# Attention kernel, 1 core: issuing the query loads and the output projection's transfers from ScalarE's instruction stream and not from SyncE's

## The chip, the cores and the metric

The kernel runs on one core of one Trainium2 chip. The metric is the device time of one execution in microseconds (us). Before the change three runs gave a median of 1577.47 us (1572.33 to 1581.16).

Five engines work beside each other, each through its own list of instructions, strictly in the order of that list: PE (TensorE, the matmuls), DVE (VectorE), ACT (ScalarE), POOL (GpSimd) and SP (SyncE, which here only starts transfers). An instruction waits for the semaphores of what it depends on, and everything behind it on its engine waits with it. A transfer (DMA) is started by an instruction of one of these lists and then moves by itself on 16 DMA engines.

## The reference

One layer: RMSNorm and one input projection, whose columns go to four mixers of width 256, then an output projection and the residual. The sequences are 2048 and 512 tokens long; the model width is 1024.

```python
def _layer(x, cos, sin, norm_w, w_in, ..., w_out):
    proj = _rms_norm(x, norm_w) @ w_in
    (a_u, a_v, a_z, b_q, ..., c_q, c_k, c_v, c_z, d_x, d_z) = _split_cols(proj)
    y_a = _sgu_mixer(a_u, a_v, sgu_w, sgu_b) * jax.nn.silu(a_z)
    y_b = _deltanet_mixer(b_q, b_k, b_v, ...) * jax.nn.silu(b_z)
    y_c = _attention_mixer(c_q, c_k, c_v, ...) * jax.nn.silu(c_z)
    y_d = _pool_mixer(d_x, pool_w, pool_scale) * jax.nn.silu(d_z)
    mix = jnp.concatenate([y_a, y_b, y_c, y_d], axis=-1)
    return x + mix @ w_out
```

The attention is softmax(q k^T / 8) v over the whole sequence, with 4 query heads on 2 key heads of width 64.

## The kernel before

Tokens are cut into five blocks of 512 (b = 0 to 3 the long sequence, b = 4 the short one). Values are carried as pairs of float16, a high part and the rest, so that one product takes three matmuls. The program has three phases that overlap. Phase 1 projects and convolves, phase 2 computes the gates and the DeltaNet recurrence, and phase 3 (line 849 on) does attention and the output projection. What a later phase needs goes through DRAM: the queries as QS, the keys as KS, the mixer outputs as MIX (eight tiles for each block).

**Attention.** Work runs over (block, head). For one head, `load_q` (L867) loads the tiles qa and qb with three transfers. `row_max` (L874) computes the row maxima: matmuls mp (L884), DVE maxima (L886), a transposing matmul mr (L892), and an ACT copy into the last row of qb (L894). `attn` (L899) then runs over the key tiles, 16 for a long block and 4 for the short one. Each key tile is one score: two matmuls into a bank sp (L909, L910), the exponential e on ACT (L912), its float16 copy p on ACT (L915), the rest of p on DVE or, for one score in four, on POOL (L916), and twelve short matmuls O (L921). While head h is in `attn`, the maxima of head h+1 are woven in, one step for each score. The tiles qa and qb have two buffers each, so the load for head h+1 has to wait until the scores of head h-1 are done. Banks of sp: three.

**Output projection.** When all four heads of a block are through, `post` finishes the DeltaNet part, and `store_mix` (L1391) writes MIX tiles: an ACT copy (L1398), a DVE rest (L1399), a store (L1400). `outproj` (L940) then issues eight loads mx of the MIX tiles (L946). Its work is queued in units: after each score `pump` takes one unit, which is three matmuls op (L958), so op fills PE between scores. For each 128 tokens there are a load of the residual xr (L952), two DVE results y (L962) and a store of y (L967).

**Order.** The order on each engine is not written by hand. A scheduler simulates the program with its own model of time and puts each instruction into its engine's list at the moment when the model has it ready, by priority: attention high, output projection low. So moving a transfer to another engine can move any instruction after it. Transfers take turns on eight completion semaphores, whichever engine starts them, and each waits for the transfer that had its semaphore before.

Of the kernel before, what the change touches and what calls it, by code (L numbers as in the profile page):

```python
# [44 lines left out]
class Trunk:  # L45
# [802 lines left out]
    def phase3(self, kp, ap, wp, ep, e5, rest, post):  # L848


        tc, nc, I = self.tc, self.nc, self.I
        V, A, G, PE, NB = nc.vector, nc.scalar, nc.gpsimd, nc.tensor, self.NB
        if True:
# [12 lines left out]
            def load_q(b, h):  # L866
                qa = ap.tile([128, 512], F16, tag="qa", name="qa")  # L867
                qb = ap.tile([65, 512], F16, tag="qb", name="qb")
                for i in range(2):
                    nc.sync.dma_start(qa[i * 64:i * 64 + 64, :], self.QS[b][0, h])  # L870
                nc.sync.dma_start(qb[0:64, :], self.QS[b][1, h])
                return qa, qb

            def row_max(seq, b, h):  # L874

                s0, n, KA, KB, vt = seq
                q = qs[b, h] = load_q(b, h)
                qa, qb = q
                nsc = n // 512
                mm = ap.tile([128, 4, nsc], F32, tag="mm", name="mm")  # L880
                for qt in range(4):
                    for sc in range(nsc):
                        mp = self.bank("M" + w0(b), [128, 512], "mp")
                        PE.matmul(mp, qa[:, qt * 128:qt * 128 + 128], KA[h // 2][:, sc * 512:sc * 512 + 512],  # L884
                                  start=True, stop=True)
                        V.tensor_reduce(mm[:, qt, sc:sc + 1], mp, axis=AX.X, op=ALU.max)  # L886
                        yield
                m16 = ap.tile([128, 4], F16, tag="m16", name="m16")
                V.tensor_reduce(m16, mm, axis=AX.X, op=ALU.max, negate=True)
                mr = self.bank("M" + w0(b), [128, 512], "mr")  # L890
                for qt in range(4):
                    PE.matmul(mr[64:65, qt * 128:qt * 128 + 128], m16[:, qt:qt + 1], self.id16,  # L892
                              start=True, stop=True, tile_position=(0, 64))
                A.activation(qb[64:65, :], mr[64:65, :], AF.Copy)  # L894
# [46 lines left out]
            def outproj(b):  # L941
                mix = []
                for f in range(8):
                    p, tag, n = (pool5(), "mx5", 7) if b % 2 and f < 7 else (ep, "mx4", 1) if b % 2 else (ep, "mx3", 8)
                    m = p.tile([128, 2, 512], F16, tag=tag, name="mx3", bufs=n)
                    nc.sync.dma_start(m, self.MIX[b][f])  # L946
                    mix.append(m)
                def units():
                    for tt in range(4):
                        t0 = b * 512 + tt * 128  # L950
                        xr = ep.tile([128, 1024], F32, tag="xr", name="xr")
                        nc.sync.dma_start(xr, I["x"][t0:t0 + 128, :])  # L952
                        y = ep.tile([128, 1024], F32, tag="y", name="y")
                        for n in range(2):
                            op = self.bank("X" + str(max(0, b - NB + 3)), [128, 512], "op")
                            for i, k in enumerate((0, 1, 6, 7, 2, 3, 4, 5)):
                                for j, (a, c) in enumerate(((0, 0), (0, 1), (1, 0))):
                                    PE.matmul(op, mix[k][:, a, tt * 128:tt * 128 + 128], wo[k][:, c, n * 512:n * 512 + 512],  # L958
                                              start=i + j == 0, stop=i == 7 and j == 2)
                                if i < 7:  # L960
                                    yield
                            V.scalar_tensor_tensor(y[:, n * 512:n * 512 + 512], op, IWS / MS, xr[:, n * 512:n * 512 + 512],  # L962
                                                   op0=ALU.mult, op1=ALU.add)
                            if n == 0:
                                yield
                        dst = self.O[0][t0:t0 + 128, :] if t0 < self.NP else self.O[1][t0 - self.NP:t0 - self.NP + 128, :]
                        nc.sync.dma_start(dst, y)  # L967
                        yield

                queue.append((clock[0] + LAG, units()))  # L970
# [3 lines left out]
            def pool5():  # L974
                if not p5:
                    p5.append(e5())
                return p5[0]
# [39 lines left out]
            for i, w in enumerate(work):  # L1017
                with tc.high_priority(offset=2000000):
                    attn(*w, row_max(*work[i + 1]) if i + 1 < len(work) else iter(()))
                if w[2] == 3:  # L1020
                    with tc.high_priority(offset=3000000):
                        post(w[1])
                    outproj(w[1])
# [462 lines left out]
```

## Time and profile before

| | |
|---|---|
| median of three runs | 1577.47 us (1572.33 to 1581.16) |
| the profiled execution | 1574.01 us |
| its span, first to last instruction | 1572.2 us |
| PE busy over the span | 1425.8 us (91%) |
| DVE | 1173.3 us (75%) |
| ACT | 797.0 us (51%) |
| POOL | 546.7 us (35%) |
| hardware DMA queue | 267.36 MB |

The busy shares are averages over phases that have different limits. Starting a transfer isn't counted as busy, so the work that the change moves is in none of these rows. In the trace, SPq stands for SP's list and PEld for the loads of weights, which overlap with PE. What stands behind "idle before" or "waited for" is the engine or transfer whose semaphore came last.

### The profile page before, as it was taken

Reading aid. Unit: us, or ns where it says so; the run is one execution under the profiler, and the core shown is the slowest. Engines: PE = TensorE matmul, PEld = TensorE weight load, DVE = VectorE, ACT = ScalarE, POOL = GpSimd, SP = SyncE. Lnnn points to the kernel's source line nnn. Section 1 sums busy time; section 2 is a strip of 40 time slices with the busy share of each in tenths; the row PEclk is TensorE's granted clock in tenths of the full one; section 3 lists DMA queues with packets and bytes.
Section 4 is the critical chain, followed back from the end, with each engine's and each line's share of the span. In section 5 each row is a group of like instructions: output and inputs, shape, how many; then the busy total and the mean of one; then the engine's idle time right before and its main releaser. Section 6 shows DMA issues by size and latency. Waiting matters only on the chain. (4 is left out here: it accounts for less than half of the span.)

```text
span 1572.2 us, 34743 instructions
## 1 busy us (share of the span) xinstructions
PE 1425.8 (91%) x13420; PEld 783.5 (50%) x13420; DVE 1173.3 (75%) x2265; ACT 797.0 (51%) x1655; POOL 546.7 (35%) x646
## 2 busy tenths in 40 slices
PE   6999999988989887987889879998799999999898
PEld 3456555543444443544445435555355555555443
DVE  6338579967969887996957769998877887877611
ACT  5244444545454844554546215565567675576400
POOL 3220220044748643455453435555121221121100
PEclk9999999998899989989999999999799999999999
DMA  9845643556566877657689885644411501414332
GB/s 254 283 168 168 190 151 114 150 194 193 160 186 201 258 234 218 199 171 215 186 259 311 278 255 177 202 139 148 161 48 39 173 34 65 160 33 135 114 128 107
DMA packets 250830, 269.65 MB, mean 172 GB/s; under 512 B 95784, under 2 KB 176680, under 8 KB 250024
## 3 DMA queue, kind: packets, MB, share of 16 engines
q1 hardware_dynamic: 250264, 267.36, 54.1%
q8 instruction: 105, 1.72, 0.4%
q14 instruction: 61, 0.50, 0.1%
q0 software_dynamic: 400, 0.07, 0.1%
HBM read 175.66 MB, written 91.77 MB: 170 GB/s over the span
## 5 line engine op out<-in xcount | busy, mean ns | idle before, releaser
L127 PEld LDWEIGHTS <-w 128*128 128x128 f16 x2280 | 223.5, 101 | 307.5 <-issue 81.8
L127 PE MATMUL accz<-xs,w 128*128 128x512 f16 x960 | 243.7, 402 | 16.8 <-DMA xs<-xs 6.7
L958 PE MATMUL op<-wo,mx 128*128 128x512 f16 x960 | 225.3, 379 | 1.0 <-DVE y L962 1.0
L886 DVE TENSOR_REDUCE mm<-mp 128x1 f32<-128x512 f32 x272 | 179.5, 683 | 52.4 <-PE mp L884 52.1
L916 POOL TENSOR_TENSOR p<-e,p 128x512 f16<-128x512 f32 x68 | 86.7, 1274 | 318.6 <-ACT p L915 283.7
L912 ACT ACTIVATE e<-sp 128x512 f32<-128x512 f32 x272 | 153.4, 596 | 79.3 <-PE sp L910 72.9
L916 DVE TENSOR_TENSOR p<-e,p 128x512 f16<-128x512 f32 x204 | 165.8, 828 | 19.3 <-ACT p L915 19.1
L127 PE MATMUL acc<-xs,w 128*128 128x512 f16 x720 | 162.8, 383 | 3.8 <-POOL xs L291 1.5
L915 ACT ACTIVATE p<-e 128x512 f16<-128x512 f32 x272 | 161.2, 632 | 3.4 <-PE O L921 2.0
L921 PEld LDWEIGHTS <-p 128*128 128x128 f16 x3264 | 128.1, 97 | 55.8 <-DVE p L916 11.2
L921 PE MATMUL O<-vt,p 128*128 128x65 f16 (+1 forms) x3264 | 142.6, 193 | 7.5 <-DVE p L916 5.3
L958 PEld LDWEIGHTS <-mx 128*128 128x128 f16 x960 | 91.3, 98 | 104.4 <-issue 1.8
L884 PE MATMUL mp<-ka,qa 128*128 128x512 f16 x272 | 98.7, 395 | 17.3 <-DVE mm L886 10.6
L909 PE MATMUL sp<-qa,ka 128*128 128x512 f16 x272 | 103.9, 384 | 2.6 <-ACT e L912 1.2
L306 DVE SCALAR_TENSOR_TENSOR cv<-raw,convw,cv 128x512 f32<-128x512 f32 x120 | 88.0, 754 | 21.2 <-POOL raw L382 20.6
L910 PE MATMUL sp<-qb,kb 65*128 65x512 f16 x272 | 100.5, 387 | 1.2 <-ACT qb L894 1.0
L127 PE MATMUL accq<-xs,w 128*128 128x512 f16 x360 | 89.5, 391 | 9.9 <-DMA xs<-xs 7.0
L400 PE MATMUL acct<-wtm,xs 128*128 128x400 f16 x480 | 83.8, 332 | 1.9 <-ACT ba L408 0.9
L1268 POOL TENSOR_TENSOR kd<-kv,kds 128x512 f16<-128x512 f32 x40 | 46.9, 1179 | 108.0 <-PE up L1305 56.0
L291 POOL TENSOR_TENSOR xs<-xt,xs 128x512 f16<-128x512 f32 x36 | 49.1, 1386 | 73.5 <-ACT xs L288 73.2
L962 DVE SCALAR_TENSOR_TENSOR y<-op,xr 128x512 f32<-128x512 f32 x40 | 27.5, 687 | 59.2 <-PE op L958 59.1
L127 PE MATMUL accu<-xs,w 128*128 128x512 f16 x240 | 60.9, 403 | 7.2 <-DVE s L616 7.0
(316 smaller groups left out, 2506.8 us busy)
## 6 DMA issues: line engine op xcount, KB each, us to landing
xs<-xs SPq DMA_DIRECT2D x120, 256.0 KB
kx<-kx SPq DMA_DIRECT2D x80, 256.0 KB
at<-at SPq DMA_DIRECT2D x80, 256.0 KB
tt<-tt SPq DMA_DIRECT2D x80, 256.0 KB
xt<-in_xT SPq DMA_DIRECT2D x40, 256.0 KB
xs<-xs SPq DMA_DIRECT2D x5, 2048.0 KB
kv<-kv SPq DMA_DIRECT2D x40, 256.0 KB
mix<-mixs SPq DMA_DIRECT2D x40, 256.0 KB
```

Source lines behind the costliest of these rows:

```text
L127: mm = self.nc.tensor.matmul(ps, w[:, a, k, :], xk, start=k + i == 0, stop=k == 7 and i == 2)
L306: V.scalar_tensor_tensor(cv, raw[:, ct, i:i + 512], self.convw[:, ct, i:i + 1], cv, op0=ALU.mult, op1=ALU.add)
L400: PE.matmul(acc[:, 0:400], xs[:, a, k, tt * 128:(tt + 1) * 128], w[:, c, k, :], start=n == 0, stop=n == 23)
L884: PE.matmul(mp, qa[:, qt * 128:qt * 128 + 128], KA[h // 2][:, sc * 512:sc * 512 + 512], start=True, stop=True)
L886: V.tensor_reduce(mm[:, qt, sc:sc + 1], mp, axis=AX.X, op=ALU.max)
L909: PE.matmul(sp, KA[kv][:, c], qa, start=True, stop=False)
L910: PE.matmul(sp, KB[kv][:, c], qb, start=False, stop=True)
L912: A.activation(e, sp, AF.Exp)
L915: A.activation(p[:, 0], e, AF.Copy)
L916: (G if st % E8 == 1 else V).tensor_tensor(p[:, 1], e, p[:, 0], op=ALU.subtract)
L921: mm = PE.matmul(O[:, qt, 0:z - a], p[:, w, q], v[:, a:z], start=st == 0 and qt == 0 and i == 0, stop=st == nst - 1 and i == 2, skip_group ...
L958: PE.matmul(op, mix[k][:, a, tt * 128:tt * 128 + 128], wo[k][:, c, n * 512:n * 512 + 512], start=i + j == 0, stop=i == 7 and j == 2)
```

## The change

Five `dma_start` calls go from `nc.sync` to `nc.scalar`: three transfers for each of the 20 heads (60), eight mx loads for each of the five blocks (40), and an xr load and a y store for each of the 20 groups of 128 tokens (20 and 20). That is 140 transfers in all. Their sizes, sources and destinations stay as they were, and the matmuls are the same.

```diff
                 for i in range(2):
-                    nc.sync.dma_start(qa[i * 64:i * 64 + 64, :], self.QS[b][0, h])
-                nc.sync.dma_start(qb[0:64, :], self.QS[b][1, h])
+                    nc.scalar.dma_start(qa[i * 64:i * 64 + 64, :], self.QS[b][0, h])
+                nc.scalar.dma_start(qb[0:64, :], self.QS[b][1, h])
                 return qa, qb
...
-                    nc.sync.dma_start(m, self.MIX[b][f])
+                    nc.scalar.dma_start(m, self.MIX[b][f])
...
-                        nc.sync.dma_start(xr, I["x"][t0:t0 + 128, :])
+                        nc.scalar.dma_start(xr, I["x"][t0:t0 + 128, :])
...
-                        nc.sync.dma_start(dst, y)
+                        nc.scalar.dma_start(dst, y)
```

Everything up to the first query load keeps its order on every engine. Behind it, the orders of all engines differ.

The first place is the end of a head on ACT, after the 176th exponential of the program. Before, ACT went from the last exponentials and copies straight to the row of the maxima (L894):

```order
L912 ACTIVATE e<-sp 128x512 x2
L915 ACTIVATE p<-e 128x512 x2
L912 ACTIVATE e<-sp 128x512
L915 ACTIVATE p<-e 128x512
L894 ACTIVATE qb<-mr 1x512
```

In the changed kernel the same place on ACT has a y store and an xr load, and then the three loads of the next head's queries:

```order
L915 ACTIVATE p<-e 128x512 x2
L967 DMA y_prompt<-y 128x1024
L912 ACTIVATE e<-sp 128x512
L952 DMA xr<-in_x 128x1024
L870 DMA qa<-qs_198 64x512 x2
L871 DMA qb<-qs_198 64x512
L915 ACTIVATE p<-e 128x512
L912 ACTIVATE e<-sp 128x512
L894 ACTIVATE qb<-mr 1x512
```

The loads now stand between one score's exponential (L912) and its copy (L915), and the store of y, which waits for PE and DVE, stands ahead of the next exponential.

The second place is the end of block 2, where the MIX tiles are written and read back. On SP before, the stores of the tiles (L1400) and the loads that wait for them (L946) stood behind each other:

```order
L1400 DMA mix_2_98<-mixs 128x1024
L1345 DMA szb<-sz_1_184 128x512
L946 DMA mx_20458<-mix_7_111 128x1024
L946 DMA mx_18625<-mix_2_98 128x1024
L933 DMA sz_20370<-sz_2_189 128x512
L1400 DMA mix_5_101<-mixs 128x1024
L1400 DMA mix_3_99<-mixs 128x1024
L967 DMA y_prompt<-y 128x1024
L952 DMA xr<-in_x 128x1024
L946 DMA mx_18627<-mix_3_99 128x1024
L946 DMA mx_18629<-mix_4_100 128x1024
```

Now the stores stay on SP, and the loads stand in ACT's list, among the exponentials and copies of the next block's first head:

```order
L967 DMA y_prompt<-y 128x1024
L952 DMA xr<-in_x 128x1024
L912 ACTIVATE e<-sp 128x512
L946 DMA mx_18627<-mix_3_99 128x1024
L912 ACTIVATE e<-sp 128x512 x2
L915 ACTIVATE p<-e 128x512
L946 DMA mx_18629<-mix_4_100 128x1024
L915 ACTIVATE p<-e 128x512
L946 DMA mx_18631<-mix_5_101 128x1024
L915 ACTIVATE p<-e 128x512
L946 DMA mx_18633<-mix_6_102 128x1024
L1332 ACTIVATE osq<-ob 128x512
```

A load such as mx<-mix_3_99 waits for the store of that tile, which SP issues, and ACT's later exponentials now wait behind it.

## The prediction

> **What bounds the kernel now.** I read the table of busy times by stage first, because a share over the whole span mixes phases. The columns are the stage, its length, and the busy time of PE, PEld, DVE, ACT and POOL with the number of instructions, then the granted clock, the DMA share and GB/s.
>
> ```profile
> 870.00:1105.00 235.00, 207.72 (x2525) 121.67 (x2524) 195.98 (x345) 110.45 (x222) 121.15 (x121) 0.96 0.63 196
> 1105.00:1200.00 95.00, 88.27 (x879) 48.03 (x878) 74.19 (x140) 56.00 (x104) 21.25 (x16) 0.92 0.29 97
> 1200.00:1440.00 240.00, 236.21 (x2481) 134.98 (x2478) 190.27 (x326) 157.42 (x295) 47.14 (x36) 0.99 0.26 87
> 1440.00:1500.00 60.00, 54.91 (x550) 30.36 (x547) 38.84 (x74) 31.07 (x59) 9.88 (x7) 1.00 0.38 125
> ```
>
> The first moved transfer is issued at 876.5 us, so nothing before it can change. From 1200 to 1440 PE is busy 236.2 of 240 us: attention there is bound by PE, since the output projection's matmuls fill the gaps. PE's idle time is 27.3 us in the first stage, 6.7 in the second, 3.8 in the third and 5.1 in the fourth. These 43 us are all that a better supply of data could win before the tail. Next I read who PE and ACT waited for between 1105 and 1500 (total us, times, longest):
>
> ```profile
> PE mp L884 <- DVE mm L886: 5.6, 10, 1.0
> PE mp L884 <- DMA qa<-qs: 2.9, 3, 1.4
> PE sp L910 <- ACT qb L894: 1.0, 2, 0.7
> PE sp L909 <- ACT e L912: 0.7, 3, 0.3
> ...
> ACT qb L894 <- PE mr L892: 56.2, 11, 11.6
> ACT e L912 <- PE sp L910: 54.9, 37, 3.9
> ```
>
> PE waits for ACT 1.7 us in 395, while ACT waits for PE 111 us. So ACT has room for more instructions as long as none of them blocks it at the wrong moment. From 870 to 1105 PE's waits for loads of queries and keys are these:
>
> ```profile
> PE mp L884 <- DMA qa<-qs: 1.8, 1, 1.8
> PE sp L909 <- DMA ka<-ks: 1.2, 1, 1.2
> PE mp L884 <- DMA ka<-ks: 0.9, 1, 0.9
> ```
>
> Last, the issues themselves (count, then least, median and greatest duration in ns of the issuing instruction on SP), and what SP waited for from 1105 to 1500:
>
> ```profile
> L870 SPq DMA_DIRECT2D qa<-qs x40: 444/551/1608, 876.5 to 1470.4; - x40
> L871 SPq DMA_DIRECT2D qb<-qs x20: 444/539/601, 877.7 to 1471.1; - x20
> L946 SPq DMA_DIRECT2D mx<-mix x40: 319/423/1654, 1105.7 to 1512.0; - x40
> L952 SPq DMA_DIRECT2D xr<-in_x x20: 376/424/576, 1107.2 to 1551.7; - x20
> L967 SPq DMA_DIRECT2D y_prompt<-y x16: 337/338/535, 1166.1 to 1534.7; - x16
> ...
> SPq L967 <- DVE y L962: 131.5, 9, 26.3
> SPq L870 <- PE sp L910: 52.4, 8, 22.1
> SPq L946 <- DMA mix<-mixs: 15.6, 10, 3.4
> ```
>
> **The change part by part.** The trace before has no transfer issued by ACT. I bound its price by the same transfer's issue on SP from above and by nothing from below, where it would run beside the activation that ACT has just started. I work with SP's medians, the nearest rows.
>
> *Query loads.* A head costs 2 x 551 + 539 ns = 1.64 us of ACT's list. The first two heads' loads fall into a stretch in which ACT idles 5.3 and then 8.7 us, and cost nothing:
>
> ```profile
> 881.47 0.60 ACT L606 ACTIVATE gz<-accz 128x512 f32<-128x512 f32 x1 [5.28 <-PE accz L127]
> 890.74 0.42 ACT L1295 ACTIVATE r<-kv 128x256 f16<-128x256 f32 x1 [8.68 <-DVE kv L1290]
> ```
>
> The other 18 heads cost 18 x 1.64 = 29.5 us. They stand between a head's last exponential and its copy p. The wait for PE is met by then, since the exponential before them already waited for the same score. What hides them is ACT's own wait right behind, for mr, 56.2 / 11 = 5.1 us each time. Queued behind them is one p, with its rest on DVE and twelve O matmuls, and PE's list has other work ahead of those. The ends are 0 and 29.5 us; I take a tenth, **+3**, near the lower end, because the row of PE waiting for ACT is 1.7 us.
>
> *Output projection.* By the changed order ACT gets 35 mx loads, 14 xr loads and 12 y stores before its last exponential: 35 x 0.423 + 14 x 0.424 + 12 x 0.338 = 24.8 us. They are spread over the scores from 1105 to 1500, of which there are 208, 395 / 208 = 1.9 us each:
>
> ```profile
> L912 ACT ACTIVATE e<-sp 128x512 f32<-128x512 f32 x208 | 116.7, 596 | 60.9 <-PE sp L910 54.9 <-DVE p L916 2.4 <-DVE m L889 0.9
> ```
>
> The cover is ACT's wait for scores, 54.9 us. The mx loads bring their waits with them: SP's 15.6 us in 10 times for the MIX stores become ACT's unless ACT arrives later. The ends are 0 and 40.4 us. I take about a tenth again, **+4**.
>
> *Waiting for y.* SP's 131.5 us were SP with nothing else to do. On ACT the store stands ahead of an exponential whose score is behind the same op matmuls in PE's list, so ACT would have waited for them anyway. New is one DVE operation between:
>
> ```profile
> L962 DVE SCALAR_TENSOR_TENSOR y<-op,xr 128x512 f32<-128x512 f32 x40 | 27.5, 687 | 59.2 <-PE op L958 59.1
> ```
>
> 12 x 0.687 = 8.2 us is the upper end, 0 the lower; I take **+1**.
>
> *What goes from SP.* PE's matmul waits for query loads are 2.9 + 1.8 = 4.7 us. Some of these loads weren't late by SP at all. At 1163.8 SP had been idle since 1144.9 and waited for PE to free the buffer, and the maxima still came 0.9 us late:
>
> ```profile
> 1144.39 0.55 SPq L871 DMA_DIRECT2D qb<-qs  x1
> 1163.82 1.08 SPq L870 DMA_DIRECT2D qa<-qs  x2
> ...
> 1166.59 0.61 PE L884 MATMUL mp<-ka,qa 128*128 128x512 f16 x2 [0.92 <-DMA qa<-qs]
> ```
>
> Others stood behind something; here it was a y store for which SP had waited:
>
> ```profile
> 1419.08 0.34 SPq L967 DMA_DIRECT2D y_prompt<-y  x1
> 1419.51 1.21 SPq L870 DMA_DIRECT2D qa<-qs  x2
> ```
>  Both ends are small, 0 and -4.7; I take **-2**. From 876.5 to 881.3 six query issues go from a list in which issues follow each other without a pause; 3.3 us is the most that the key loads behind them can gain. PE's waits for key loads are 1.2 + 0.9 us, so I take **-1**.
>
> [...]
>
> *Order.* Behind 876.5 the scheduler has put everything anew, and 27.3 us of PE idle in the first stage can grow or shrink. I see no sign in the order lists: PE still has one three-matmul unit behind most scores, and the tail behind the last O matmul holds 324 op matmuls where it held 336. I take 0, with 8 us to either side.
>
> Sum: 3 + 4 + 1 - 2 - 1 = **+5 us** on the profiled execution's 1574.0, so 1579.0. That execution is 3.5 us below the median of three; from the median the sum is 1582.5. I predict **1580 us**, between them and within 0.5% (7.9 us, about what a measurement of this kernel can tell from no change).
>
> **The rivals.**
>
> *Slower: ACT blocked at the block ends.* There ACT has no idle time. From 1435.7 to 1449.5 its rows follow without a gap longer than 1 us:
>
> ```profile
> 1435.72 0.60 ACT L912 ACTIVATE e<-sp 128x512 f32<-128x512 f32 x1
> ...
> 1445.34 0.63 ACT L1398 ACTIVATE mixs<-szb 128x512 f16<-128x512 f32 x1 [0.98 <-DVE szb L1350]
> ...
> 1448.91 0.62 ACT L1332 ACTIVATE osq<-ob 128x512 f32<-128x512 f32 x1
> ```
>
> Into such stretches go 35 mx issues (14.8 us), their waits (15.6 us) and four heads' loads (6.6 us): 37 us. It decides as soon as ACT is late by more than two scores, 3.8 us, since PE has three banks and then stands still. A block end gets 37 / 4 = 9 us within some 14 us, so half may pass: +18, with the other terms +20, so **1594**, and 1611 if all of it does. Against it stand ACT's 54.9 us of waiting for scores, and that the scheduler put each load where its model had the store landed.
>
> *Faster: SP was the late one.* SP starts 140 transfers less, about 65 us of issue, and what stays on it (recurrence, gates, MIX stores) comes earlier. If all the waits named above go, -4.7 - 3.3, and PE's wait for gate inputs below goes too, the gain is 14.4 us, less 3 for ACT: **1563**, or 1566 from the median.
>
> ```profile
> PE accz L127 <- DMA xs<-xs: 6.4, 5, 1.5
> ```
>
> Against it: only 18 of the moved transfers are issued before 1100, where the recurrence runs, and those that remain wait for PE, DVE and POOL in most rows. [...]
>
> *The change doesn't do what it says.* Each transfer still waits for the one that had its semaphore before, on whichever engine, so the loads come no earlier, and ACT's issues all fall into its 111 us of waiting. Then the time stays at **1574 to 1578**.
>
> **How the numbers follow.** Forecast 40%, slower rival 30%, faster rival 15%, nothing at all 15%. Slower by over 0.5% (above 1585.4) is the slower rival and a little of the forecast's upper edge: 0.34. Faster (below 1569.6) is the faster rival and the order's luck: 0.17. Within 0.5%: 0.49. The range for 8 in 10 goes from 1566, the faster rival from the median, to 1602, beyond the slower rival's middle.
>
> **What would show it.** Query loads right: PE's waits for qa stay at 2 to 5 us, and ACT's wait for mr falls by about 1.6 us a head while PE stays over 97% busy in its attention middle. Output projection wrong: PE's waits for e, p or qb grow from 2 to over 10 us, and they stand at the block ends, with ACT idle in front of mx loads and released by a MIX store. Faster rival: PE idle before 1105 falls below 20 us. An ACT issue far from 0.3 to 0.55 us would upset the first two terms alike, and a changed idle time before 1105 without any of these waits would be the new order.

## The result and the profile after

The changed kernel takes **1565.36 us** (median of 20 runs, 1560.73 to 1571.70) against 1572.62 us of the kernel before (20 runs, 1568.40 to 1581.16): a ratio of **0.9942**, 95% interval 0.9928 to 0.9955, so 0.6% faster. The prediction was 1580 us, range 1566 to 1602: wrong in sign, and the time lies just below the range. Its base was high too: the three runs of before that it knew had a median of 1577.47, 4.9 us above that of the twenty.

The profiled execution after took 1570.22 us, with a span of 1568.4; it is 3.8 us faster than the profiled execution before, where the medians differ by 7.3. First the table by stage, in the same stages as before (PE, PEld, DVE, ACT and POOL busy with their instructions, then clock, DMA share and GB/s):

```profile
870.00:1105.00 235.00, 207.80 (x2532) 120.96 (x2529) 198.55 (x366) 109.24 (x222) 122.91 (x122) 0.99 0.65 205
1105.00:1200.00 95.00, 92.63 (x1002) 52.57 (x1003) 80.43 (x135) 65.89 (x123) 22.11 (x16) 1.00 0.21 69
1200.00:1440.00 240.00, 229.51 (x2426) 131.22 (x2423) 182.92 (x315) 153.99 (x287) 44.41 (x35) 0.99 0.27 90
1440.00:1500.00 60.00, 55.92 (x481) 29.75 (x480) 35.45 (x71) 26.49 (x49) 8.23 (x6) 0.95 0.37 120
```

PE's idle time up to 1105 is what it was, 27.2 us. The second stage is the new one: 1002 matmuls where there were 879, at a clock of 1.00 where it was 0.92. From 1200 to 1440 PE is idle 10.5 us, and it was 3.8: some of what was won is given back there. Next, whom PE and ACT waited for from 1105 to 1500:

```profile
PE O L921 <- DVE p L916: 2.9, 5, 2.1
PE mp L884 <- DVE mm L886: 2.5, 5, 0.8
PE sp L909 <- ACT e L912: 2.1, 4, 0.6
PE op L958 <- DMA mx<-mix: 2.0, 2, 1.7
PE sp L910 <- ACT qb L894: 1.9, 2, 1.6
...
PE O L921 <- ACT p L915: 1.7, 2, 1.4
...
ACT e L912 <- PE sp L910: 57.8, 39, 5.0
ACT qb L894 <- PE mr L892: 26.5, 7, 13.3
```

PE no longer waits for a query load there, its wait for the maxima (L886) has halved, and ACT's wait for mr fell from 56.2 to 26.5 us. New is the wait for an mx load, and PE's waits for ACT (e, qb and p) grew from 1.7 to 5.7 us. The issues on ACT cost about what they cost on SP, where the medians were 551, 423 and 424 ns (least, median and greatest duration in ns):

```profile
L870 ACTq DMA_DIRECT2D qa<-qs x40: 452/482/1167, 873.4 to 1468.5; - x40
L946 ACTq DMA_DIRECT2D mx<-mix x40: 321/354/1308, 1092.3 to 1510.4; - x40
L952 ACTq DMA_DIRECT2D xr<-in_x x20: 339/446/1823, 1094.9 to 1546.7; - x20
```

The first mx load is issued at 1092.3 where it was 1105.7. That is 13.4 us sooner, before any transfer of the output projection has moved, so the place to look at is the boundary between blocks 0 and 1.

### The boundary of blocks 0 and 1

Block 0 has 64 scores. PE issues two more first halves (L909), for the next head, and then needs that head's row of maxima; "the gap behind the 66th score" is the time until the next L909. These are rows of PE's timeline of the kernel before, with one of DVE's and one of ACT's; the bracket is the idle time before the row and what ended it:

```profile
1090.63 0.38 PE L909 MATMUL sp<-qa,ka 128*128 128x512 f16 x1
...
1102.14 0.58 PE L884 MATMUL mp<-ka,qa 128*128 128x512 f16 x1 [3.27 <-DVE mm L886]
1103.07 0.80 PE L1312 MATMUL up<-v,at 128*128 128x64 f16 x12 [0.35 <-DVE S L1307]
...
1110.41 0.59 PE L884 MATMUL mp<-ka,qa 128*128 128x512 f16 x1 [0.78 <-DVE mm L886]
1111.79 1.97 PE L1348 MATMUL tpo<-ident,ob 128*128 128x128 f32 x8 [0.79 <-POOL ob L1342]
...
1117.46 0.63 PE L909 MATMUL sp<-qa,ka 128*128 128x512 f16 x1
...
1100.80 0.69 DVE L1333 TENSOR_REDUCE om<-osq 128x8 f32<-128x512 f32 x1 [2.50 <-ACT osq L1332]
...
1100.14 0.63 ACT L1332 ACTIVATE osq<-ob 128x512 f32<-128x512 f32 x1 [2.73 <-DMA ob<-od]
```

The gap is 26.8 us. In it three things share the lists: the last steps of the recurrence (its last matmuls, L1312, end at 1103.9), the closing work on block 0's recurrence output (`post`: L1332 to L1350), and the 16 maxima of the next head. DVE stood 2.50 us for a square of ACT (L1332) with maxima queued behind it, and PE stood 3.27 us for those. The square itself had waited for the load of the recurrence's output (ob). Within PE's wait the clock fell to half, as the windows show, and a 128x512 matmul takes 0.58 to 0.63 us where it took 0.38:

```profile
1098.00:1102.00 4.00, 0.84 (x13) 0.51 (x13) 1.50 (x3) 1.63 (x3) 0.00 (x0) 0.73 0.48 172
1102.00:1106.00 4.00, 2.39 (x15) 1.04 (x15) 3.74 (x10) 0.15 (x1) 0.72 (x1) 0.50 0.51 181
1106.00:1110.00 4.00, 1.76 (x3) 0.31 (x3) 3.69 (x16) 0.00 (x0) 0.17 (x1) 0.50 0.84 259
...
1114.00:1118.00 4.00, 3.86 (x13) 1.38 (x13) 3.04 (x5) 2.95 (x6) 0.00 (x0) 0.50 0.75 238
...
1102.00:1118.00 16.00, 10.81 (x40) 4.44 (x40) 12.44 (x33) 3.37 (x7) 2.62 (x2) 0.50 0.69 230
```

In these 16 us PE was busy 10.81 at half clock, work of 5.4 us: the L909 and L910 that follow each other from 1117.46 to 1118.74, at 0.50, start 0.43 us apart, and the 128x512 matmuls from 1124.63 to 1125.71, at 1.00, 0.22 us.

The same place on PE in the changed kernel:

```profile
1087.71 0.51 PE L1312 MATMUL up<-v,at 128*128 128x64 f16 x12
1094.02 0.38 PE L909 MATMUL sp<-qa,ka 128*128 128x512 f16 x1
1097.14 4.44 PE L127 MATMUL accu<-xs,w 128*128 128x512 f16 x12 [0.65 <-DVE gz L607]
1106.88 0.38 PE L909 MATMUL sp<-qa,ka 128*128 128x512 f16 x1 [0.27 <-DVE szb L1350]
```

The recurrence has ended 15.7 us earlier, at 1088.2, its closing work begins among the last scores of block 0 (its squares at 1077.6 and 1080.4, before at 1100.1 and 1101.5), gate matmuls (L127) fill the gap, and the gap lasts 12.9 us. One row of the windows for each kernel, before and then after, says what that is worth:

```profile
1100.00:1120.00 20.00, 12.81 (x46) 5.17 (x46) 15.64 (x37) 5.12 (x9) 3.77 (x3) 0.50 0.60 200
...
1100.00:1120.00 20.00, 18.76 (x157) 9.41 (x156) 17.92 (x32) 13.34 (x26) 3.56 (x4) 0.97 0.57 193
```

46 matmuls at clock 0.50 became 157 at 0.97. The recurrence is ahead long before the boundary: at 1000 us the kernel before has 12 of its steps left (counted by the ends of L1312), the changed one nine. Before, the last steps of its two chains come in pairs (they end at 1071 and 1071, then 1090 and 1091, then 1104), after, one at a time (1055, 1064, 1069, 1078, 1088). That this is why it is ahead isn't shown: in q_not1 below they come one at a time too (1061, 1070, 1079, 1086, 1098) and end late.

### The profile page after: what moved, and what is told of

Same layout as the page of the kernel before. It is cut to its first block, busy times and chain, and to the rows that moved or that the text cites. A ratio compares the mean times of both kernels' runs of the same rounds, so it can differ in the third digit from the quotient of the medians.

```text
span 1568.4 us, 34669 instructions
## 1 busy us (share of the span) xinstructions
PE 1421.8 (91%) x13420; PEld 781.9 (50%) x13420; DVE 1170.1 (75%) x2265; ACT 798.8 (51%) x1655; POOL 548.0 (35%) x646
## 4 chain that ended last, share of the span: by engine, by line
PE 30%; DVE 14%; DMA 10%; issue 2%; ACT 2%; POOL 1%; SPq 1%; ACTq 0%; DVEq 0%
PE op L958 12%; PE O L921 4%; PE accz L127 3%; DVE mm L886 2%; PE sp L910 2%; PE sp L909 2%; DVE p L916 2%; PE mp L884 2%; PE accu L127 2%; DMA xs<-xs 1%; DVE ltmp L1153 1%; DMA kv<-kv 1%; DMA qs<-q 1%; DMA wst<-in_w_out 1%; DVE lx L1154 1%
## 5 line engine op out<-in xcount | busy, mean ns | idle before, releaser
L127 PEld LDWEIGHTS <-w 128*128 128x128 f16 x2280 | 224.1, 101 | 308.8 <-issue 80.9
L127 PE MATMUL accz<-xs,w 128*128 128x512 f16 x960 | 243.9, 403 | 18.1 <-DMA xs<-xs 10.7
L912 ACT ACTIVATE e<-sp 128x512 f32<-128x512 f32 x272 | 155.0, 597 | 92.0 <-PE sp L910 72.3
L886 DVE TENSOR_REDUCE mm<-mp 128x1 f32<-128x512 f32 x272 | 179.7, 682 | 29.4 <-PE mp L884 28.5
L915 ACT ACTIVATE p<-e 128x512 f16<-128x512 f32 x272 | 162.9, 635 | 23.1 <-issue 6.7
L127 PE MATMUL acc<-xs,w 128*128 128x512 f16 x720 | 163.6, 384 | 3.1 <-ACT xs L288 1.5
L909 PE MATMUL sp<-qa,ka 128*128 128x512 f16 x272 | 103.7, 383 | 3.7 <-ACT e L912 3.1
L910 PE MATMUL sp<-qb,kb 65*128 65x512 f16 x272 | 99.8, 384 | 2.4 <-ACT qb L894 2.2
L127 PE MATMUL accq<-xs,w 128*128 128x512 f16 x360 | 86.1, 380 | 9.7 <-DMA xs<-xs 6.9
L127 PE MATMUL accu<-xs,w 128*128 128x512 f16 x240 | 61.3, 407 | 8.0 <-DVE s L616 7.2
```

Source lines behind the costliest of these rows:

```text
L127: mm = self.nc.tensor.matmul(ps, w[:, a, k, :], xk, start=k + i == 0, stop=k == 7 and i == 2)
L909: PE.matmul(sp, KA[kv][:, c], qa, start=True, stop=False)
L910: PE.matmul(sp, KB[kv][:, c], qb, start=False, stop=True)
L912: A.activation(e, sp, AF.Exp)
L915: A.activation(p[:, 0], e, AF.Copy)
```

## The experiments

Theories: **order** (the gain is the recurrence's earlier end, a product of the scheduler's new order, wherever the transfers are issued), **sooner queries** (the loads themselves come earlier for every head), **freed SP** (SP no longer waits for mix and y ahead of other transfers). Each kernel was timed in five rounds against the kernel before on the same chip.

### The change in pieces

q_only moves L870 and L871 alone, out_only L946, L952 and L967 alone. q_b0 and q_rest move the query loads of some blocks, here q_b0 (L871 likewise; q_rest has `b > 0`):

```diff
-                    nc.sync.dma_start(qa[i * 64:i * 64 + 64, :], self.QS[b][0, h])
+                    (nc.scalar if b == 0 else nc.sync).dma_start(qa[i * 64:i * 64 + 64, :], self.QS[b][0, h])
```

> Only the query loads (L870, L871) go to ACT; mx, xr and y stay on SP. The whole change gave 0.9942, 7.3 us. Order theory (the gain is the new order of recurrence, gates and block 0 that the moved loads bring about, before the first mx load): the program is the changed one up to the first output projection, so 0.993 to 0.997, 5 to 11 us less. Theory of sooner queries (the loads themselves come earlier for all 20 heads): the same, 0.993 to 0.997. Theory of a freed SP (what counts is that SP no longer has to wait for mix and y ahead of other transfers): 0.999 to 1.001.

> The query loads of block 0 alone (4 heads of 20) go to ACT, the other 16 heads' and the output projection's stay on SP. Order theory: recurrence and block 0 have nearly the changed order, so most of the gain, 0.994 to 0.997. Theory of sooner queries: 4 heads of 20, a fifth of 7.3 us, 0.998 to 1.000. Theory of a freed SP: 0.999 to 1.001.

> The query loads of blocks 1 to 4 (16 heads of 20) go to ACT, block 0's stay on SP; the order of PE is that of before until block 1. Order theory: the recurrence is as before, so nothing, 0.999 to 1.001. Theory of sooner queries: 16 heads of 20, 0.994 to 0.997. Theory of a freed SP: 0.999 to 1.001.

> Only the output projection's transfers (L946, L952, L967) go to ACT; all query loads stay on SP. Order theory: the recurrence is as before and ACT pays for the issues, so 0.999 to 1.003. Theory of sooner queries: some loads no longer stand behind y stores, 0.998 to 1.001. Theory of a freed SP: most of the gain, 0.993 to 0.997.

Measured: q_only 0.9952 (0.9931 to 0.9972), **q_b0 0.9906** (0.9874 to 0.9937), **q_rest 1.0008** (0.9984 to 1.0031), **out_only 1.0032** (1.0010 to 1.0054). Four heads' loads bring the whole gain, sixteen heads' bring none, and the output projection's transfers cost 0.3%. The product 0.9906 x 1.0008 x 1.0032 = 0.9946 is the whole change's 0.9942. Freed SP (which had out_only at 0.993 to 0.997) and sooner queries (which had q_rest there) fall; the order theory alone fits, with q_b0 better than it had said and out_only 0.0002 above its range. Where the order in front of block 1 is the old one, the boundary looks as before: first q_rest, then out_only.

```profile
1100.00:1120.00 20.00, 13.47 (x55) 5.85 (x53) 15.46 (x39) 5.23 (x9) 4.18 (x3) 0.58 0.51 168
...
1100.00:1120.00 20.00, 11.47 (x43) 4.72 (x42) 14.49 (x36) 5.12 (x9) 3.27 (x3) 0.61 0.64 213
```

### The same order by other means, and another order by the same means

None of v_act, kb_act and qa3 moves a transfer of the change. v_act issues the five loads of V from ACT, kb_act the loads of the keys' second part, qa3 gives the query tiles a third buffer. q_not1 moves the query loads of 19 heads (in q_b0's line the condition is `b + h > 0`), q_first those of the first head alone (`b == 0 and h == 0`).

```diff
-                    nc.sync.dma_start(vt[:, b].rearrange("p t k d -> p t (k d)"), self.VT[s0 // 512 + b])
+                    nc.scalar.dma_start(vt[:, b].rearrange("p t k d -> p t (k d)"), self.VT[s0 // 512 + b])
...
-                        nc.sync.dma_start(kb[0:64, c], kd[0, kv])
+                        nc.scalar.dma_start(kb[0:64, c], kd[0, kv])
...
-                qa = ap.tile([128, 512], F16, tag="qa", name="qa")
+                qa = ap.tile([128, 512], F16, tag="qa", name="qa", bufs=3)
```

> No transfer of the change is moved; instead the five loads of V (L994) go to ACT. By the order of the instructions the recurrence's last matmul stands behind the 62nd score, as in the changed kernel. Order theory: most of the gain, 0.992 to 0.997, and the gap behind the 66th score falls from 27 to 9 to 15 us. Theory of sooner queries: they come as before, 0.999 to 1.001.

> No transfer of the change is moved; instead the loads of the keys' second part (L1004) go to ACT. The recurrence's last matmul stands behind the 50th score, 12 further ahead than in the changed kernel. Order theory: at least the gain of the change, 0.988 to 0.996; if only the distance from the boundary counts, no more than the best so far, 0.990 to 0.994. Theory of sooner queries: 0.999 to 1.001.

> No transfer changes its engine: all stay on SP; the query tiles qa alone get a third buffer. By the order of the instructions the recurrence's last matmul stands behind the 62nd score (before: 66th) and block 1's output projection begins behind the 140th, both as in the changed kernel. Order theory: the time of the changed kernel without any ACT issue, 0.992 to 0.997, and the gap behind the 66th score 9 to 15 us. If the engine of the query loads counts: 0.998 to 1.002.

> The query loads of 19 heads go to ACT, only the very first head's stay on SP; mx, xr and y stay on SP. By the order of the instructions the recurrence's last matmul still stands behind the 66th score of block 0 and 1, as before (in the changed kernel behind the 62nd), so it falls on the boundary between the two blocks. Order theory: no gain, 0.998 to 1.002, the gap between the 66th score and the next stays above 18 us. Theory of sooner queries (ACT issues them earlier for each head): 19 heads of 20, 0.993 to 0.997.

> The query loads of the first head alone (3 transfers) go to ACT. They leave SP's list at its busiest place, before the first key loads; but by the order of the instructions the recurrence's last matmul stands behind the 66th score and block 1's output projection begins behind the 146th, both as before. Order theory: 0.998 to 1.002 and a gap above 18 us. If relief of SP's list at 876 us is the cause: 0.992 to 0.997.

| kernel | recurrence ends (us) | gap behind the 66th score | clock 1100 to 1120 | ratio (95% interval) |
|---|---|---|---|---|
| before | 1103.9 | 26.8 | 0.50 | 1 |
| changed | 1088.2 | 12.9 | 0.97 | 0.9942 (0.9928 to 0.9955) |
| q_only | 1088.9 | 11.2 | 1.00 | 0.9952 (0.9931 to 0.9972) |
| q_b0 | 1086.2 | 8.9 | 0.83 | 0.9906 (0.9874 to 0.9937) |
| v_act | 1084.5 | 12.9 | 1.00 | 0.9932 (0.9913 to 0.9952) |
| qa3 | 1090.7 | 11.4 | 1.00 | 0.9985 (0.9971 to 1.0000) |
| kb_act | 1081.9 | 10.4 (behind the 68th) | 1.00 | 1.0010 (0.9993 to 1.0027) |
| q_rest | 1102.5 | 20.0 | 0.58 | 1.0008 (0.9984 to 1.0031) |
| out_only | 1105.0 | 26.9 | 0.61 | 1.0032 (1.0010 to 1.0054) |
| q_not1 | 1098.2 | 24.9 | 0.74 | 0.9966 (0.9950 to 0.9982) |
| q_first | 1108.0 | 16.7 | 0.76 | 0.9966 (0.9949 to 0.9984) |

v_act has the gain with every transfer of the change on SP, and its row of the boundary is much like the changed kernel's:

```profile
1100.00:1120.00 20.00, 18.75 (x169) 9.74 (x167) 19.99 (x33) 15.09 (x29) 5.76 (x4) 1.00 0.51 163
```

Every kernel whose recurrence ends by 1091 has a gap of 8.9 to 12.9 us and a clock of 0.83 or more there; that half of the order theory held in all six. The other half, that this sets the time, is only partly right, and four expectations missed. kb_act has the boundary but pays ahead of it: its scores 16 to 48 come 13 to 25 us later than before. qa3 has it (10 us of lead at 1200) and loses it all at the next boundary. q_not1 and q_first gained 0.3% where nothing was expected, with a recurrence that ends late; q_first's gap of 16.7 us was to stay above 18. q_not1's time lies where sooner queries had it, and q_first's where a relief of SP's list at 876 us had it. Sooner queries fell with q_rest; the relief alone didn't end the recurrence earlier in q_first, but that it is worth some time isn't excluded. That third of a per cent has no place in these traces that I can name; q_first's own can't show it, since the profiled execution took 1574.56 us where the median of its runs is 1569.82.

To say where a lead is won and lost, I summed each kernel's matmuls, weighted by the full-clock time of their shape, and looked when it had as much of them left as the kernel before had at a given time. Negative is ahead, in us; one execution each, so 2 us are nothing:

| kernel | 1080 | 1115 | 1200 | 1300 | end |
|---|---|---|---|---|---|
| changed | 0.8 | -11.5 | -14.0 | -7.1 | -3.9 |
| q_only | 1.2 | -12.3 | -16.1 | -5.9 | -3.0 |
| q_b0 | 0.1 | -14.6 | -13.3 | -7.3 | -9.3 |
| v_act | 1.9 | -11.9 | -15.3 | -10.7 | -13.6 |
| qa3 | 6.9 | -8.3 | -10.1 | 0.0 | 1.0 |
| q_rest | 5.8 | 0.3 | -1.6 | 4.6 | 4.9 |
| out_only | 0.4 | -0.2 | 1.1 | 4.5 | 6.1 |

The lead arises between 1080 and 1115, 12 to 15 us of it in the first five. Not all of it is the one gap: some 3 us arise between 1080 and 1085, where PE in the kernel before waited 1.69 us for the recurrence (L1300) and then ran at half clock (0.50 from 1082.9 to 1086.2). From 1200 to 1300, at the boundary of blocks 1 and 2, every kernel of the table gives back 3 to 10 us.

### The closing work alone

post_late leaves all transfers on SP and holds block 0's closing work back until the seventh score of the next head:

```diff
+                    if st == 6 and late:
+                        bb = late.pop()
+                        with tc.high_priority(offset=1000000), tc.issue_after(pa.ins):
+                            post(bb)
+                        outproj(bb)
```

> All transfers stay on SP and the recurrence is in the order of before; only the closing work on block 0's recurrence output (post: squares, row sums, inverse root, transposes), with the output projection of block 0 behind it, is held back until the seventh score of the next head. If the gain comes from taking that work off the boundary (DVE's list and the PSUM bank that its transposes hold), the gap behind the 66th score falls from 27 to 12 to 18 us and the ratio is 0.992 to 0.997. If the recurrence's own last steps at the boundary are what costs, the gap stays above 20 us and the ratio is 0.998 to 1.002.

The time is **1.0063** (1.0042 to 1.0083), slower than either theory had it, and the gap decides for neither. It is 7.9 us behind the 66th score, but only because PE issues a third first half there; behind the 67th another 14.2 us follow. Between the second halves (L910) of the 64th and the 65th score lie 22.3 us, where the kernel before has 27.0 and the changed one 17.7. So taking the closing work away is worth 4.7 of the 9.3 us by which the changed kernel is better there. And that work only moved: behind the 74th score a second gap opens, of 18.3 us, with the clock low again. The second stretch of post_late, and PE's longest wait from 1110 to 1145 (its lines there stand seven lower in the file, so L1355 is L1348):

```profile
1120.00:1140.00 20.00, 8.60 (x51) 4.05 (x50) 13.23 (x33) 3.65 (x7) 3.55 (x2) 0.64 0.38 118
...
PE tpo L1355 <- POOL ob L1349: 6.9, 1, 6.9
```

So the boundary as a place isn't all that costs. The closing work's chain through ACT, DVE and POOL ends in PE's transposes, and here PE stood at them until the chain was through.

### The next boundary

In q_only PE waited 3.6 us there for an mx load; first its wait, then the row on its timeline, then the same wait in qa3:

```profile
PE op L958 <- DMA mx<-mix: 3.6, 1, 3.6
...
1240.38 6.62 PE L958 MATMUL op<-wo,mx 128*128 128x512 f16 x18 [3.62 <-DMA mx<-mix]
...
PE op L958 <- DMA mx<-mix: 4.1, 1, 4.1
```

The 18 matmuls behind it took 6.62 us, where 18 times the 0.216 us of full clock (256 of them take 55.42 us at the end of the kernel before, at 1.00) are 3.9. In the order of the instructions block 1's output projection begins behind the 140th score in q_only, qa3, the changed kernel and q_rest, behind the 146th in the kernel before, where PE's wait for mx at this place is missing. So I held it back:

```diff
-                queue.append((clock[0] + LAG, units()))
+                queue.append((clock[0] + (16 if b == 1 else LAG), units()))
```

> As q_only, but the output projection of block 1 is held back until 16 scores behind its block's end, not 4 (L970, block 1 alone). The order of PE is that of q_only until then. In q_only its first matmuls stand behind the 140th score (before: behind the 146th), and there PE waited 3.6 us for an mx load with the clock at 0.72 behind it, and about 8 us of the lead were gone. If that early place is what gives the lead back: the mx wait goes, PE is over 9.5 us of 10 busy from 1230 to 1260, and the ratio falls from 0.9952 to 0.990 to 0.994, since some 2 to 3 us come back as output projection behind the last score. If the issues on ACT give it back: 0.995 to 0.998.

> The whole change, with the output projection of block 1 held back to 16 scores behind its block's end. Recurrence as in the changed kernel. If the early place of block 1's output projection gives back part of the lead, the mx wait (1.7 us) and the clock drop at 1240 go and the ratio is 0.991 to 0.994; the issues of mx, xr and y on ACT stay and cost what they cost (out_only 1.0032). If not: 0.994 to 0.997.

> q_b0 (block 0's query loads on ACT, 0.9906) with the output projection of block 1 held back to 16 scores behind its block's end. In q_b0 that place cost little (3 to 4 us of the lead gone by 1300, 10 us in q_only). If the early place always gives lead back, 0.987 to 0.990; if it did so only where PE waited for mx, as in q_only and qa3, no more than q_b0: 0.990 to 0.994.

q_only_w16 came out in its range, 0.9921 (0.9904 to 0.9939), with the mx wait gone, though its interval overlaps that of q_only. after_w16 did not: 0.9971 (0.9954 to 0.9988), if anything worse than the changed kernel, though its mx wait is gone too. q_b0_w16 gave 0.9948 (0.9926 to 0.9970), not better than q_b0. The early place goes with q_only's wait, but what the changed kernel gives back isn't explained by it; that stays open.

### The clock

warm is the kernel before with the 16 maxima matmuls of block 1's first head issued three times each, warm_twice with two:

```diff
-                        PE.matmul(mp, qa[:, qt * 128:qt * 128 + 128], KA[h // 2][:, sc * 512:sc * 512 + 512],
-                                  start=True, stop=True)
+                        for _ in range(3 if (b, h) == (1, 0) else 1):
+                            PE.matmul(mp, qa[:, qt * 128:qt * 128 + 128], KA[h // 2][:, sc * 512:sc * 512 + 512],
+                                      start=True, stop=True)
```

> The kernel before, all transfers on SP, with the 16 maxima matmuls of block 1's first head (the ones that run in the gap behind the 66th score) each issued three times with the same result: 32 more matmuls, 7 us of PE at 0.215 us each, in a place where PE waits. The recurrence still ends behind the 66th score. If a large part of what the boundary costs is the granted clock (0.50 from 1102 to 1119 in the kernel before, where 15.7 us of matmuls ran at 0.50 to 0.73), the clock there stays above 0.9 and the added work is paid back: 0.996 to 1.001. If the clock is only a side effect, or falls all the same: 1.002 to 1.006, the 7 us less what the gap hides.

> As warm, but each of the 16 maxima matmuls of block 1's first head is issued twice, not three times: 16 more matmuls, 3.4 us of PE; all transfers on SP, the recurrence's end in its old place. In warm the granted clock stayed at 1.00 through the boundary; the time that its missing clock stands for, (1 - mean clock) x time over the runs, was 53 us against 65 in the kernel before, and the rest of the time 8.6 us more. If the clock at the boundary is the price and half as many matmuls still hold it: 12 us less and some 4 more, 0.993 to 0.997. If fewer don't hold it: 0.999 to 1.004.

warm: **0.9994** (0.9975 to 1.0013), with 7 us of work added. warm_twice: 0.9992 (0.9970 to 1.0014); there the clock fell all the same, to 0.58 at 1102. In warm it stayed full, with PE little more than half busy and a gap of 26.1 us, nearly as long as before. A full clock, then, doesn't close the gap (the added matmuls stand in it too):

```profile
1098.00:1102.00 4.00, 2.16 (x19) 0.99 (x18) 3.93 (x11) 0.00 (x0) 0.72 (x1) 1.00 0.68 202
1102.00:1106.00 4.00, 2.20 (x9) 0.86 (x9) 2.87 (x12) 0.00 (x0) 0.42 (x1) 1.00 0.94 287
```

Every timed run reports its mean granted clock, so the time splits into (1 - clock) x time, the most that the missing clock can have cost, and the rest. Medians over the runs, in us; the kernels before are those timed beside each:

| kernel | missing clock | the rest | before: missing clock | the rest |
|---|---|---|---|---|
| changed (20 runs) | 50.2 | 1515.0 | | |
| q_b0 (6) | 49.2 | 1514.1 | 63.1 | 1511.4 |
| q_only (12) | 51.9 | 1514.5 | 63.1 | 1511.4 |
| out_only (12) | 67.2 | 1514.9 | 63.1 | 1511.4 |
| q_rest (12) | 63.9 | 1513.7 | 63.1 | 1511.4 |
| v_act (6) | 52.3 | 1508.9 | 66.1 | 1509.8 |
| kb_act (12) | 59.7 | 1518.2 | 66.1 | 1509.8 |
| qa3 (12) | 58.2 | 1513.9 | 61.4 | 1512.3 |
| q_not1 (12) | 64.4 | 1505.9 | 66.1 | 1509.8 |
| q_first (12) | 60.6 | 1509.8 | 61.4 | 1512.3 |
| post_late (6) | 70.5 | 1513.0 | 66.1 | 1509.8 |
| warm (12) | 53.4 | 1518.9 | 65.3 | 1510.3 |

In q_b0, q_only and v_act 11 to 14 us of missing clock go, and the rest of the time doesn't fall by more than 1 us. That is the upper end of the clock's share, since it counts the clock that is missing while PE waits too (0.65 over the wait of 3.27 us in the kernel before). No lower end is shown: between 1102 and 1118 5.4 us of matmul work took twice as long, but PE also stood 0.39 to 1.04 us for DVE's maxima (L886) ahead of five of the matmuls mp there, and a faster matmul may only have waited longer. In kb_act and qa3, which have the boundary but not the gain, 6 and 3 us of missing clock go and the rest is 8.4 and 1.6 us longer. The small gains of q_not1 and q_first lie for the most part in the rest and not in the clock. warm bought 12 us of clock with 8.6 us of other time, nearly its 7 us of matmuls: the clock can be had there with nothing else changed, though hardly for less than it brings.

### Both reliefs together

v_q_b0 has the edits of q_b0 and of v_act: block 0's query loads and the loads of V from ACT.

> Block 0's query loads and the loads of V together on ACT. By the order of the instructions the recurrence's last matmul stands behind the 58th score (q_b0 60th, V alone 62nd, kb 50th). If the gain of the boundary is had once the recurrence is out of its way, no more than either alone, 0.990 to 0.994, or less if attention pays ahead of the boundary as it did with kb (12 to 24 us late at scores 16 to 48, 1.001). If reliefs add up: 0.984 to 0.989.

0.9921 (0.9892 to 0.9949): the reliefs don't add up, though at this boundary no gap over 5.1 us is left between two first halves. No kernel here is shown to beat q_b0 (1563.38 us, median of 6 runs), whose interval overlaps that of the changed kernel.

## Why the prediction was wrong

- **Order, 0 with 8 us to either side: this step failed.** "I see no sign in the order lists" looked at the units behind the scores and at the tail. The sign was in them: the recurrence's last matmul moved from behind the 66th score to behind the 62nd, out of the boundary. The runs showed a lead of 12 to 15 us in its place, most of it in the one gap, where PE's matmuls ran at half clock; part of it was given back later, and by the medians 7.3 us are left. v_act shows that this needs none of the moved transfers; q_rest and out_only, that the moved transfers without it bring nothing. Which part of the new order sets the time is argued from gap, clock and lead and not isolated: kb_act and qa3 have the early recurrence and no gain, and q_not1 and q_first gain 0.3% without it.
- **PE idle in the first stage** was taken as the measure of the faster rival (below 20 us). It stayed at 27 us; the gain lay behind it. Nor were PE's 43 us of idle time all that could be won: its busy time held matmuls at half clock. The table by stage had shown the place, 0.92 of the clock from 1105 to 1200, and the prediction didn't ask why.
- **Query loads, +3.** Not contradicted, and not shown: 16 of the 20 heads cost 0.08% (-0.16 to 0.31%), 1.3 us, which can't be told from nothing.
- **Output projection +4 and waiting for y +1.** Right in size: out_only costs 0.32%, 5.0 us (1.6 to 8.5). Its trace fits the mechanism, with PE's waits for ACT from 1105 to 1500 at 5.9 us (before 1.7), but its missing clock is 4.1 us more as well, so the agreement may be in part luck.
- **What goes from SP, -2 and -1.** The order of size is right, the view wrong that the qa waits would stay at 2 to 5 us: they fell from 4.7 to 0.5 us, and those for keys from 2.1 to 1.0. Whether SP's shorter list ended these waits isn't shown, since the order changed with it.
- **Slower rival, ACT blocked at the block ends.** Its place exists: all kernels of the lead table lose 3 to 10 us from 1200 to 1300. Its cause isn't settled, since q_only and qa3 lose most there and have no mx load on ACT.
- **Faster rival.** Its time, 1563 to 1566, was right by another mechanism, which is luck. SP being late had little to do with it: v_act leaves all 140 transfers on SP, and in qa3, where no transfer leaves SP, the recurrence ends early too. PE's wait for gate inputs, which this rival was to end, rose from 6.4 to 10.7 us.

## What to carry to other kernels

Where a scheduler places the instructions, moving a DMA start to another engine is first of all a new order, and that can be worth more than the issues: here a lead of 12 us against the 5 us that the output projection's transfers cost. So read the static order at the places where two stages meet, and look which chain ends there and what stands behind it in the lists of PE and DVE. A mean clock below 1 in a stage can hide such a place, as 0.92 did here; find where it falls (here 1.0 us into a wait of PE), and count the matmuls at 0.50 at double their time, as measured here: 128x512 matmuls 0.43 us apart and not 0.22.

## What the hardware showed

The clock can fall before a wait of PE is over and stay low for longer than the wait. In the kernel before it fell at 1099.9 us, 1.0 us into the wait of 3.27 us, behind 3.4 us in which PE was busy 47%. It then stayed at half for 20.4 us, in windows in which PE was busy 44 to 97% (1.76 and 3.86 of 4 us in the rows above). First the 3.4 us ahead of the fall, then the wait, then the stretch at half clock:

```profile
1096.46:1099.87 3.41, 1.59 (x28) 0.97 (x27) 1.62 (x3) 0.38 (x1) 0.72 (x1) 1.00 0.58 193
1098.87:1102.14 3.27, 0.00 (x1) 0.00 (x1) 1.34 (x3) 1.77 (x3) 0.00 (x0) 0.65 0.36 124
1099.87:1120.30 20.43, 13.12 (x47) 5.33 (x47) 15.94 (x37) 5.12 (x9) 3.77 (x3) 0.50 0.61 203
```

In warm the clock stayed at 1.00 in windows in which PE was busy 54 and 55%. The busy time of such windows alone doesn't tell the cases apart: in the changed kernel the clock fell for 3.4 us (0.50 from 1097.75 to 1101.10) without a wait over 0.73 us, behind a window that was 59% busy:

```profile
1094.00:1098.00 4.00, 2.37 (x19) 1.08 (x19) 4.00 (x8) 0.97 (x2) 0.00 (x0) 0.97 0.91 279
1098.00:1102.00 4.00, 4.00 (x22) 1.59 (x20) 1.06 (x3) 0.00 (x0) 0.00 (x0) 0.61 0.99 389
```

Half and full are what these windows show: 1.00 ahead of the fall and 0.50 behind it. In the kernel before the clock came back at 1120.3, behind 3.4 us in which PE was busy throughout. It had fallen behind 3.4 us that were 47% busy, and in the changed kernel behind a window of 4 us that was 59% busy. What decides whether it falls isn't shown by these runs.
